# Twenty-six projection blocks of a hybrid layer computed as thirteen pairs of seven block products, with the gate pairs moved between the recurrence's heads

## The chip, the cores and the metric

The kernel runs as one program on one core of one Trainium2 chip. The core has five engines that take their instructions in order, each from its own queue: TensorE (PE, with its weight loads shown apart as PEld), VectorE (DVE), ScalarE (ACT), GpSimd (POOL) and SyncE (SP, which here only issues DMAs). They wait for one another through semaphores. The metric is the device time of one execution in microseconds (us), as the median of several runs.

## The reference

One residual layer over 512 tokens and 16 prepended meta tokens, model width 2048, all in float32.

```python
h = rms_norm(x, norm_g);  proj = h @ w_in          # w_in is 2048 x 12368
(q_a, k_a, v_a, z_a, q_i, k_i, w_i, q_b, f_b, i_b, z_b, gates) = split(proj)
...                                                 # branch A: indexer, top-128 keys per query, attention
y_a = o_a * silu(z_a)
qb = silu(q_b);  f = lb + (1 - lb) * sigmoid(f_b);  vb = i_b
o_b = hgrn2_chunkwise(qb, 1 - f, vb, log f)         # S_t = diag(f_t) S_{t-1} + k_t v_t^T, o_t = S_t^T q_t
y_b = rms_norm(o_b) * silu(z_b)
p = einsum('btnc,ncd->btnd', [y_a, y_b], w_branch)
out = x + sum_n(sigmoid(gates_n) * p_n) @ w_out
```

Branch B has 8 heads of 128 channels. Per head it needs one 128-column block each of q_b, f_b, i_b and z_b. The f and i blocks are needed for the meta tokens too (528 tokens), q and z for the 512 tokens alone.

## The kernel before, in words

**Layout.** The normalised input h is kept transposed in SBUF, 16 tiles of 128 channels by 528 tokens, each as a pair: hH (h rounded to the fast float32r format) and hL (the rest). Every weight chunk of 128 x 1024 numbers (`raw`, a 512 KB DMA on SP's queue; six buffers) is split in the same way into `wh` by an ACT copy and `wl` by a DVE subtraction (function `hi_lo`, three buffers of each). A product is then three matmuls per 128 x 128 weight block: hH with wh, hL with wh, hH with wl.

**Two kinds of projection.** A plain job (`Job`) makes one block of 128 output columns: 16 channel tiles x 3 matmuls of 512 tokens, or, where the meta tokens are needed (k, v, f, i), 16 x 3 matmuls of 264 tokens twice. A `Pair` makes two blocks together by a scheme in Winograd's form of Strassen's algorithm: the weight matrix of the two blocks is a 2 x 2 of sub-matrices (two output blocks by two halves of the channels, raw chunks 11, 21, 22, 12), the tokens are cut into two halves, and seven block products of 8 x 3 matmuls of 256 tokens replace eight. It needs four sums of weight chunks, s1 to s4 (`sum_1` ... `sum_4`), sums of the input halves (`tops_task`, once for all pairs, into the tiles TB; `place_t3` writes one more into h's own tiles), and five additions of products in `run_pair` (the p1, g1 and g2 tiles; PSUM banks px, py, pz, pw). Of the input projection only the merge gates are made in pairs (16 of them); the output projection is made in 8 pairs (`run_out`).

**Order.** One loop goes through the list `jobs`: indexer, z_a, k, v, q of attention, then per head of the recurrence q, f, i (24 plain jobs), then 8 plain z_b jobs, 16 gate pairs, 32 branch jobs, 8 output pairs. Everything that isn't a projection runs as generators (`ki_task`, `idx_task`, `topk_task`, `qa_task`, `pv_task`, `hgrn_task`, `gate_task`, `tops_task`): after every three matmuls of a plain job `pump` lets those continue whose results a small clock in the kernel's own planner (`Core`, costs in ns) holds to be ready. So the planner writes down one fixed order for each engine. Before the first gate pair all tasks are finished, and `run_pair` pumps none.

**The recurrence.** `hgrn_task` runs a head as a chain: transposes of v (bank phv), the diagonal product (phd), then seven levels. A level is 16 (at the end 8 and 4) small matmuls into the bank phl, then on DVE a predicated copy into `attn`, a product into k (`hk`), one into q (`QA`) and one into the decays (`TT`). The next level's matmuls wait for `hk` and `QA`. Then come the state products (phk, phs, `S`), the output (pho), its norm with a power on POOL (`hsq`), and in `gate_task` a transpose and the product with silu(z).

**Splits.** The chunk for product i+3 is split when product i is over, since three buffers stand in a ring; so it has the time of two products before PE needs it.

Of the kernel before, what the change touches and what calls it, by code (L numbers as in the profile page):

```python
# [16 lines left out]
D = 2048  # L17
# [20 lines left out]
LAT = 180.0  # L38
SAME = {"pe": 0.0, "act": 60.0, "dve": 125.0, "pool": 60.0}
MARGIN = 300.0  # L40


class Core:
# [63 lines left out]
    def ptt(self, out, a, b, op):  # L107
        self.nc.gpsimd.tensor_tensor(out, a, b, op=op)  # L108
# [66 lines left out]
def hybrid_kernel(ctx, tc, x, meta, vecs, w_in, rows, w_branch, w_out,  # L175
# [8 lines left out]
    S = Slots(E, sp, [f"s{i}" for i in range(67)], [128, T], None)  # L184
# [87 lines left out]
    vrow = cp.tile([35, 128], F32, name="vrow")  # L272
# [7 lines left out]
    RB = cp.tile([128, 192], F32, name="RB")  # L280
    tabA = cp.tile([128, 5, 64], F32, name="tabA")
    tabI = cp.tile([128, 5, 32], F32, name="tabI")
# [40 lines left out]
    class Pair:  # L323
# [3 lines left out]
        def __init__(self, kind, c0, c1, k0, k1, nk, ncols, n=0, done=None, more=()):  # L327
            self.kind, self.c0, self.n, self.done, self.nk, self.ncols = kind, c0, n, done, nk, ncols
            self.meta, self.pre, self.req, self.more = False, None, None, more
# [115 lines left out]
    def consts():  # L445
# [42 lines left out]

    def prep(half, kt):
# [42 lines left out]
    wi = cp.tile([128, 4, 16], F32, name="wi")  # L532
# [59 lines left out]
    def idx_task(j, xq):  # L592
# [50 lines left out]
        if not idx_left[0]:  # L643
            S.put(kkH, kkL, CQ, SQ)
# [100 lines left out]
    zs = {}  # L745
    yd = [[tc.dram_tile([128, 512], F32, name=f"yd{n}_{h}") for h in range(8)] for n in range(2)]

    def spill_y(n, h, s, e):
        yield e
        nc.sync.dma_start(yd[n][h], s[:, :512])  # L750
# [5 lines left out]
    def qa_task(h, xq, prev):  # L756
# [24 lines left out]
        for qt in (3, 2, 1, 0):  # L781
# [6 lines left out]
            else:  # L788
                pb = yield from bank("plg")
                parts = [(pb[:, :kq], slice(0, kq))]  # L790
                vs[qt] = pb[:, :kq]
# [10 lines left out]
        for qt in (3, 2, 1, 0):  # L802
# [5 lines left out]
            (B2 if kq > 512 else B1).put(pbs[qt])  # L808
# [12 lines left out]
    def pv_task(h, ps, e):  # L821
# [7 lines left out]
        po = yield from bank("pov")  # L829

# [15 lines left out]
        for b in (3, -1, 0, 1, 2):  # L846
# [13 lines left out]
            B1.put(pb)  # L860
            if b != 2:
# [15 lines left out]
        e = E.tt(zs[h][:, :512], po, zs[h][:, :512], OP.mult)  # L877
        B1.put(po)
        spawn(spill_y(0, h, zs[h], e), 0)
# [9 lines left out]
    AT = [None, None]  # L889
# [741 lines left out]
```

## Time and profile before

| | |
|---|---|
| median of 3 runs | 1587.43 us (1586.98 to 1587.56) |
| the profiled execution's own time | 1591.29 us |
| its span from the first instruction to the last | 1589.5 us |
| granted TensorE clock | 0.998 |
| busy: PE, PEld, DVE, ACT, POOL | 1569.0, 1425.6, 1058.0, 592.4, 73.0 us |
| heads of the recurrence (first q block to last head) | about 490 to 830 us |
| z_b jobs | about 830 to 928 us |
| 16 gate pairs | about 928 to 1246 us |
| branch jobs | about 1246 to 1426 us |
| output pairs | about 1426 to 1589 us |

In a group's row of the profile stand the line, the engine, the operation, what is written and read, and the count; then busy us, mean ns of one, idle time of the engine just before them, and what ended it. Line numbers are those of the kernel that ran; most operations are recorded by helpers, so one line (L104: DVE's tensor_tensor; L90 and L88: matmuls) stands for many places, and the tile names tell them apart.

### The profile page before, as it was taken

The numbers are of one execution on the slowest core, as the hardware profiler recorded it, in microseconds if no ns is written. First come the engines' busy times: TensorE is split into PE (matmuls) and PEld (weight loads), VectorE is DVE, ScalarE is ACT, GpSimd is POOL, SyncE is SP. The second block draws the span as 40 slices with busy tenths as digits, with TensorE's granted clock in tenths as the row PEclk, the third lists the DMA queues.
The fourth block names the chain that finished last, engine by engine and source line by source line (L and its number), as shares of the span: only waits on it lengthen the run. The fifth ranks groups of instructions, "written<-read, shape, count | busy, mean of one in ns | idle before, by whom it ended". The sixth has DMA issues, their size and how long they took to land.

```text
span 1589.5 us, 28143 instructions
## 1 busy us (share of the span) xinstructions
PE 1569.0 (99%) x11736; PEld 1425.6 (90%) x11736; DVE 1058.0 (67%) x1821; ACT 592.4 (37%) x922; POOL 73.0 (5%) x63
## 2 busy tenths in 40 slices
PE   7999999999999999999999999999999999999998
PEld 6888889998879888999997899999999888889998
DVE  6687899526665645444445887777777543779886
ACT  5555322334444322222222344444444331334332
POOL 3100000100000000000000000000000000002111
PEclk9999999999999999999999999999999999999999
DMA  9222333333223222323232434444445764444551
GB/s 256 80 67 80 86 102 85 90 82 86 61 67 93 69 80 67 81 67 80 68 80 80 120 99 133 132 134 132 134 126 139 233 198 136 144 130 142 163 161 55
DMA packets 277904, 175.76 MB, mean 111 GB/s; under 512 B 8660, under 2 KB 263136, under 8 KB 277776
## 3 DMA queue, kind: packets, MB, share of 16 engines
q1 hardware_dynamic: 272208, 167.58, 37.4%
q10 hardware_dynamic: 5504, 6.29, 1.2%
q8 instruction: 92, 1.51, 0.4%
q14 instruction: 36, 0.29, 0.1%
q0 software_dynamic: 64, 0.08, 0.0%
HBM read 157.16 MB, written 16.78 MB: 109 GB/s over the span
## 4 chain that ended last, share of the span: by engine, by line
PE 95%; DVE 2%; issue 1%; DMA 1%; ACT 1%; POOL 0%; SPq 0%; ACTq 0%; DVEq 0%
PE pg L90 58%; PE po L88 9%; PE px L88 6%; PE py L88 6%; PE pz L88 5%; PE pw L88 3%; PE phl L90 1%; PE psc L90 1%; PE plg L90 1%; PE pov L88 1%; PE pho L90 1%; PE ppt L94 1%; PE px L94 1%; DVE wl L104 0%; PE phd L90 0%
## 5 line engine op out<-in xcount | busy, mean ns | idle before, releaser
L104 DVE TENSOR_TENSOR wl<-raw,wh 128x1024 fp32r<-128x1024 f32 x276 | 340.6, 1234 | 208.2 <-ACT wh L98 207.8
L90 PE MATMUL pg<-hH,wh 128*128 128x264 f32 (+1 forms) x1392 | 478.2, 344 | 0.0
L98 ACT ACTIVATE wh<-raw 128x1024 fp32r<-128x1024 f32 x278 | 294.2, 1058 | 483.0 <-PE pg L90 243.5
L90 PE MATMUL pg<-hH,wl 128*128 128x264 f32 (+1 forms) x1392 | 464.3, 334 | 0.0
L90 PE MATMUL pg<-hL,wh 128*128 128x264 f32 (+1 forms) x1392 | 462.7, 332 | 0.0
L90 PEld LDWEIGHTS pg<-hH,wl 128*128 128x128 f32 x1392 | 261.7, 188 | 26.4
L90 PEld LDWEIGHTS pg<-hH,wh 128*128 128x128 f32 x1392 | 261.7, 188 | 22.1 <-ACT hv L98 0.2
L90 PEld LDWEIGHTS pg<-hL,wh 128*128 128x128 f32 x1392 | 262.2, 188 | 21.3
L88 PE MATMUL po<-wh,mh 128*128 128x256 f32 x896 | 159.1, 281 | 0.7 <-DVE xq L104 0.5
L88 PEld LDWEIGHTS po<-wh,mh 128*128 128x128 f32 x896 | 137.5, 189 | 1.1 <-DVE xq L104 0.7
L88 PE MATMUL po<-wl,mh 128*128 128x256 f32 x448 | 125.7, 281 | 0.0
L90 PE MATMUL pg<-yH,wh 128*128 128x512 f32 x256 | 101.1, 395 | 0.4 <-ACT yH L98 0.4
L90 PE MATMUL pg<-yL,wh 128*128 128x512 f32 x256 | 100.7, 393 | 0.4 <-DVE yL L104 0.3
L90 PE MATMUL pg<-yH,wl 128*128 128x512 f32 x256 | 100.8, 394 | 0.0
L88 PEld LDWEIGHTS po<-wl,mh 128*128 128x128 f32 x448 | 84.3, 188 | 0.2
L98 ACT ACTIVATE wh<-sum 128x1024 fp32r<-128x1024 f32 x48 | 51.0, 1062 | 84.7 <-DVE wl L104 24.8
L104 DVE TENSOR_TENSOR wl<-sum,wh 128x1024 fp32r<-128x1024 f32 x48 | 61.8, 1287 | 16.9 <-ACT wh L98 16.9
L88 PE MATMUL px<-hL,wh 128*128 128x256 f32 x256 | 72.3, 282 | 0.0
L88 PE MATMUL px<-hH,wl 128*128 128x256 f32 x256 | 72.2, 282 | 0.0
L88 PE MATMUL px<-hH,wh 128*128 128x256 f32 x256 | 71.9, 281 | 0.0
L108 POOL TENSOR_TENSOR xq<-xq,op 128x512 f32<-128x512 f32 x16 | 30.4, 1914 | 689.1 <-ACT op L98 671.8
L90 PEld LDWEIGHTS pg<-yL,wh 128*128 128x128 f32 x256 | 48.2, 188 | 12.2 <-DVE yL L104 1.1
(310 smaller groups left out, 2626.8 us busy)
## 6 DMA issues: line engine op xcount, KB each, us to landing
raw<-in_w_in_dram SPq DMA_DIRECT2D x192, 512.0 KB, 3.9
raw<-in_w_branch_dram SPq DMA_DIRECT2D x32, 512.0 KB, 4.3
raw<-in_w_out_dram SPq DMA_DIRECT2D x32, 512.0 KB, 3.6
gd<-gate SPq DMA_DIRECT2D x32, 256.0 KB, 4.3
g<-gd SPq DMA_DIRECT2D x30, 256.0 KB, 3.0
x<-in_x_dram SPq DMA_DIRECT2D x16, 256.0 KB, 5.7
xq<-in_x_dram ACTq DMA_DIRECT2D x16, 256.0 KB, 4.0
out_dram<-xq SPq DMA_DIRECT2D x15, 256.0 KB, 2.4
```

Of the source, the lines that this page charges most:

```text
L88: self.nc.tensor.matmul(out, lhsT, rhs, start=start, stop=stop, skip_group_check=True)
L90: self.nc.tensor.matmul(out, lhsT, rhs, start=start, stop=stop)
L94: self.nc.tensor.transpose(out, in_, ident)
L98: self.nc.scalar.activation(out, in_, f, **kw)
L104: self.nc.vector.tensor_tensor(out, a, b, op=op)
L108: self.nc.gpsimd.tensor_tensor(out, a, b, op=op)
```

## The change

- The q, f and i blocks of all eight heads and the last two z_b blocks are made in pairs by the seven products: f with i of one head (8 pairs, half width 264 tokens, since each half takes 8 meta tokens along), q with q of two heads (3 pairs), z with q (2 pairs). The first six z_b blocks stay plain jobs and come before them.
- The 16 gate pairs no longer follow the heads: two of them stand after each head's f and i pair. `run_pair` now pumps tasks after every three matmuls, and the tasks are no longer finished before the first pair; only `tops_task` is. It is cut in two, starts at the seventh q_a job of the attention in place of the fourth z_b job, and waits for free slots.
- h's columns are laid out as two halves of 264 tokens (8 meta and 256 others each), so plain jobs of 512 tokens read two stretches of 256.
- The weight sums s3 and s4 are no longer DVE additions but DMAs issued by POOL that add into the destination (`dma_add`), for all 37 pairs, the output's too; s4 is issued one product earlier than before.
- silu(z_a) and silu(z_b) are written to DRAM and read back (SP's queue) where they are used, and some tables share the general slots, of which there are 69 in place of 67.
- One `attn` tile in place of two; a pair of a head's q, f, i goes through SBUF (p1, g1, g2) instead of being read from PSUM.

```diff
+NSLOT = 69
+    def dma_add(self, out, a):
+        self.nc.gpsimd.dma_start(out, a, accum_op=OP.add)
+        return self.at("pool", 4000.0, [out], [out, a])
...
     def sum_3(pr):
             pr.s3 = pr.raw["21"]["raw"]
-            E.tt(pr.s3, pr.raw["11"]["raw"], pr.s3, OP.add)
+            E.dma_add(pr.s3, pr.raw["11"]["raw"])
     def sum_4(pr):
             pr.s4 = pr.raw["12"]["raw"]
-            E.tt(pr.s4, pr.s2, pr.s4, OP.add)
+            E.dma_add(pr.s4, pr.s2)
...
     def hgrn_task(h, prev):
         while (prev and not prev.done) or not all(t.done for t in qa_tasks):
             yield WAIT
+        while not all(i in hg[h] for i in ("q", "k", "v")):
+            yield WAIT
+        yield hg[h]["t"]
...
+        while len(S.free) < 3:
+            yield WAIT
...
     def gate_task(h, on):
-        while "z" not in hg[h]:
+        while not S.free or "z" not in hg[h]:
             yield WAIT
-        z = hg[h]["z"]
+        z = slot("hz")
+        nc.sync.dma_start(z[:, :512], zd[h])
...
-        yield e
+        yield e + 3000.0
...
     def d_za(h):
         def f(b):
-            zs[h] = silu_mul(b, "zs")
+            s = silu_mul(b, "zs")
+            spawn(spill(zad[h], s, E.clk["dve"] + LAT), 0)
...
+    def d_zp(h):
+        def f(g):
+            s, e = silu(g, "hz")
+            hg.setdefault(h, {})["z"] = 1
+            spawn(spill(zd[h], s, e), 0)
...
-    def tops_task():
+    def tops_task(i):
-        for k in range(8):
+        for k in range(4 * i, 4 * i + 4):
+            while len(S.free) < 8 + ROOM or k > 3 and k - 4 not in TB:
+                yield WAIT
...
     def run_pair(pr, nxt, late, last):
-        bk, W = {}, slice(0, 256)
+        w = pr.w
+        bk, W, V = {}, slice(0, w), slice(w, 2 * w)
...
             for k in range(8):
-                th, tl = TB[k][tn]
+                th, tl = (t[:, 264 - w:264] for t in TB[k][tn])
                 E.mm(b, op["h"][k], th, st_, False, loose=True)
                 E.mm(b, op["h"][k], tl, False, False, loose=True)
                 E.mm(b, op["l"][k], th, False, k == 7, loose=True)
+                pump()
...
-            elif i == 2:
+            if i == 1:
                 sum_4(pr)
...
-    for h in range(8):
-        jobs += [Job("in", C_QB + 128 * h, 128, done=d_qb(h)), Job("in", C_FB + 128 * h, 128, True, done=d_fb(h)),
-                 Job("in", C_IB + 128 * h, 128, True, done=d_ib(h))]
-    jobs += [Job("in", C_ZB + 128 * h, 128, done=d_zb(h)) for h in range(8)]
-    jobs[-5].pre = pre_t
+    jobs += [Job("in", C_ZB + 128 * h, 128, done=d_zb(h)) for h in range(6)]
+    jobs[-8].pre = pre_t
...
+    Q, Z = ([(c + 128 * h, d(h)) for h in range(8)] for c, d in ((C_QB, d_qb), (C_ZB, d_zp)))
+    first = [(Z[6], Q[0]), (Z[7], Q[1]), (Q[3], Q[2]), None, (Q[5], Q[4]), None, (Q[7], Q[6]), None]
+    gates = [(n, j) for n in range(2) for j in range(0, 16, 2)]
     for h in range(8):
+        if first[h]:
+            two(*first[h])
+        two((C_FB + 128 * h, d_fb(h)), (C_IB + 128 * h, d_ib(h)), w=264)
+        for n, j in gates[2 * h:2 * h + 2]:
+            c = C_G + D * n + 128 * j
+            two((c, d_gate(n, j, 256)), (c + 128, d_gate(n, j + 1, 0)), f=AF.Sigmoid)
...
-                for t in hg_tasks + on_tasks + t_task:
+                for t in t_task:
                     finish(t)
-                while tasks:
-                    finish(tasks[0])
```

The order of the built program shows the rest at three places. On DVE, at the middle levels of a head: before, in the fifth head, stand the level's four operations (`attn`, `hk`, `QA`, `TT`), and of the projection that runs beside them one product with the sigmoid (`hq`) and splits (`wl`):

```order
L942 COPY_PREDICATED attn_4863<-masks,phl_5282 128x32x8
L104 TENSOR_TENSOR hk_7013<-hk_7013,TT_7177 128x33x8
L104 TENSOR_TENSOR QA_7161<-QA_7161,TT_7177 128x32x8
L104 TENSOR_TENSOR TT_7177<-TT_7177 128x33
L104 TENSOR_TENSOR hq_7319<-pg_7144,hq_7319 128x512
L104 TENSOR_TENSOR wl_7325<-raw_6863,wh_7324 128x1024
L942 COPY_PREDICATED attn_4863<-masks,phl_5282 128x16x16
L104 TENSOR_TENSOR hk_7013<-hk_7013,TT_7177 128x16x16
L104 TENSOR_TENSOR QA_7161<-QA_7161,TT_7177 128x16x16
L104 TENSOR_TENSOR TT_7177<-TT_7177 128x16
L942 COPY_PREDICATED attn_4863<-masks,phl_5282 128x8x32
```

Now, in the same head, beside a gate pair (`p`, `g`: additions of products; `sum`: s1 and s2 of the next pair):

```order
L976 COPY_PREDICATED attn_6082<-masks,phl_6089 128x64x4
L106 TENSOR_TENSOR hk_10248<-hk_10248,TT_10310 128x66x4
L106 TENSOR_TENSOR QA_10282<-QA_10282,TT_10310 128x64x4
L106 TENSOR_TENSOR TT_10310<-TT_10310 128x66
L106 TENSOR_TENSOR g_546_10449<-p_539_10234,pz_10404 128x256
L106 TENSOR_TENSOR sum_150_10451<-sum_150_10396,raw_10078 128x1024
L106 TENSOR_TENSOR wl_10454<-raw_10078,wh_10453 128x1024
L976 COPY_PREDICATED attn_6082<-masks,phl_6089 128x32x8
L106 TENSOR_TENSOR hk_10248<-hk_10248,TT_10310 128x33x8
L106 TENSOR_TENSOR QA_10282<-QA_10282,TT_10310 128x32x8
L106 TENSOR_TENSOR TT_10310<-TT_10310 128x33
L106 TENSOR_TENSOR g_546_10449<-p_539_10234,pw_10457 128x256
```

Between two levels DVE now has an addition of products, a weight sum and a split, where it had at most a sigmoid product and a split.

On PE, at the turn of a product in a head's levels, stand before three matmuls of 512 tokens per channel tile (bank pg), and the level (phl) after nine of them:

```order
L90 MATMUL phl_5282<-QA_6231,hk_6083 32x16 x16
L90 MATMUL pg_6214<-hH_396,wh_6087 128x512
L90 MATMUL pg_6214<-hL_397,wh_6087 128x512
L90 MATMUL pg_6214<-hH_396,wl_6088 128x512
L90 MATMUL pg_6214<-hH_413,wh_6157 128x512
L90 MATMUL pg_6214<-hL_414,wh_6157 128x512
L90 MATMUL pg_6214<-hH_413,wl_6158 128x512
L90 MATMUL pg_6214<-hH_429,wh_6157 128x512
L90 MATMUL pg_6214<-hL_430,wh_6157 128x512
L90 MATMUL pg_6214<-hH_429,wl_6158 128x512
L90 MATMUL phl_5282<-QA_6231,hk_6083 32x16 x16
```

Now the level stands between the products of a gate pair (banks py, pz), matmuls of 256 tokens. The end of one such gap, in the fourth head:

```order
L90 MATMUL py_9152<-hH_388,wh_9137 128x256
L90 MATMUL py_9152<-hL_389,wh_9137 128x256
L90 MATMUL py_9152<-hH_388,wl_9138 128x256
L90 MATMUL py_9152<-hH_412,wh_9137 128x256
L90 MATMUL py_9152<-hL_413,wh_9137 128x256
L90 MATMUL py_9152<-hH_412,wl_9138 128x256
L90 MATMUL pz_9306<-tT_4606,wh_9188 128x256
L90 MATMUL pz_9306<-tT_4607,wh_9188 128x256
L90 MATMUL pz_9306<-tT_4606,wl_9189 128x256
L92 MATMUL phl_6089<-QA_9184,hk_9150 32x16 x16
```

From the first level of that head to the last, the six gaps hold 21, 18, 30, 27, 18 and 21 of these matmuls.

On POOL stand, in the stretch of the heads and gate pairs, before only the powers of the heads' norms, one for each head:

```order
L108 TENSOR_TENSOR hsq_6579<-hsq_6579,mhalf 128x4
L108 TENSOR_TENSOR hsq_7044<-hsq_7044,mhalf 128x4
L108 TENSOR_TENSOR hsq_7509<-hsq_7509,mhalf 128x4
L108 TENSOR_TENSOR hsq_7974<-hsq_7974,mhalf 128x4
L108 TENSOR_TENSOR hsq_8439<-hsq_8439,mhalf 128x4
```

Now the adding DMAs of two weight sums for every pair stand among them (`raw<-raw`: s3 of the next pair; `raw<-sum`: s4 of the running one):

```order
L110 TENSOR_TENSOR hsq_7651<-hsq_7651,mhalf 128x4
L115 DMA raw_7338<-raw_7283 128x1024
L115 DMA raw_7539<-sum_110_7709 128x1024
L115 DMA raw_7679<-raw_7629 128x1024
L115 DMA raw_7818<-sum_114_7946 128x1024
L115 DMA raw_7917<-raw_7882 128x1024
L115 DMA raw_8047<-sum_118_8176 128x1024
L115 DMA raw_8147<-raw_8112 128x1024
L115 DMA raw_8275<-sum_122_8485 128x1024
L110 TENSOR_TENSOR hsq_8749<-hsq_8749,mhalf 128x4
```

So between the powers that two heads' norms wait for, POOL here issues eight such DMAs.

More of the change, by code (lines that the diff above doesn't have):

```diff
@@ L183, in hybrid_kernel @@
     E = Core(nc)
-    S = Slots(E, sp, [f"s{i}" for i in range(67)], [128, T], None)
+    S = Slots(E, sp, [f"s{i}" for i in range(NSLOT)], [128, T], None)
     B1 = Slots(E, pp, [f"b{i}" for i in range(6)], [128, 512], None)
@@ L487, in hybrid_kernel, with halves, tok @@
     hH, hL = [], []
+    def halves(a):
+        return a[:, :528].rearrange("p (a b) -> p a b", a=2)
+    def tok(b):
+        o = 128 * b + (8 if b < 2 else 16)
+        return slice(o, o + 128)
     def prep(half, kt):
@@ L788, in qa_task @@
             else:
-                pb = yield from bank("plg")
-                parts = [(pb[:, :kq], slice(0, kq))]
-                vs[qt] = pb[:, :kq]
+                if qt:
+                    pb = yield from bank("plg")
+                vs[qt] = pb[:, :kq] if qt else pb[:, KQ[1]:KQ[1] + kq]
+                parts = [(vs[qt], slice(0, kq))]
             pbs[qt] = pb
@@ L888, in hybrid_kernel @@
     on_tasks = []
-    AT = [None, None]
+    AT = []
+    zd = [tc.dram_tile([128, 512], F32, name=f"zd{h}") for h in range(8)]
     MT = cp.tile([128, 256], F32, name="MT")
+    VM = [cp.tile([128, 16], F32, name=f"VM{i}") for i in range(2)]
     LB = []
@@ L1199, in run_pair @@
             if i == 2:
-                g1, g2 = slots("gate", 2)
-                pr.done(0, g1[:, W], b, None)
+                g1 = main_slot("g1")
+                E.act(g1[:, W], b, pr.f)
                 B1.put(bk["x"])
             elif i == 5:
-                late.append(lambda g=g2: pr.done(1, g[:, :512], g[:, :512], g))
+                late.append(lambda g=g2: pr.done[1](g))
             elif i == 6:
-                late.append(lambda g=g1: pr.done(0, g[:, 256:512], g[:, 256:512], g))
+                late.append(lambda g=g1: pr.done[0](g))
             if last:
@@ L1398, in pre_t @@
     def pre_t():
-        t_task.append(spawn(tops_task(), 2))
+        t_task.extend(spawn(tops_task(i), 2) for i in range(2))
     def req_br(n, p):
@@ L1512, in hybrid_kernel @@
     for ji, job in enumerate(jobs[2:], 3):
-        need[0] = 1 + jobs[ji].meta if ji < len(jobs) else 0
+        need[0] = 1 + (jobs[ji].meta or "pair" in (job.kind, jobs[ji].kind)) if ji < len(jobs) else 0
         if job.pre:
@@ L1517, in hybrid_kernel @@
             job.req()
-        if job.kind == "gate":
+        if job.kind == "pair":
             npair += 1
             if npair == 1:
-                for t in hg_tasks + on_tasks + t_task:
+                for t in t_task:
                     finish(t)
-                while tasks:
-                    finish(tasks[0])
                 late += [lambda: place_t3(0), lambda: place_t3(4)]
@@ L1545, in hybrid_kernel @@
             b = B1.get("pg")
[L1546 removed]
+            parts = [(b[:job.ncols, :], slice(0, 512))]
+            if job.kind == "in":
+                parts = [(b[:job.ncols, :].rearrange("p (a b) -> p a b", a=2), None)]
         for ch in job.chunks:
@@ L1555, in hybrid_kernel @@
                 for o, c in parts:
-                    mm3(o, ch, kk_, kt, mh[:, c], ml[:, c], kt == 0, kt == job.kts - 1)
+                    u, v = (t[:, c] if c else halves(t)[:, :, 8:264] for t in (mh, ml))
+                    mm3(o, ch, kk_, kt, u, v, kt == 0, kt == job.kts - 1)
                 pump()
```

183 lines of the change are left out of this document (108 added, 75 removed).

## The prediction

> **What bounds the kernel now.** I read the page's busy times and its chain first:
>
> ```profile
> PE 1569.0 (99%) x11736; PEld 1425.6 (90%) x11736; DVE 1058.0 (67%) x1821; ACT 592.4 (37%) x922; POOL 73.0 (5%) x63
> PE 95%; DVE 2%; issue 1%; DMA 1%; ACT 1%; POOL 0%; SPq 0%; ACTq 0%; DVEq 0%
> PE pg L90 58%; PE po L88 9%; PE px L88 6%; PE py L88 6%; PE pz L88 5%; PE pw L88 3%; PE phl L90 1%; PE psc L90 1%; PE plg L90 1%; PE pov L88 1%; PE pho L90 1%; PE ppt L94 1%; PE px L94 1%; DVE wl L104 0%; PE phd L90 0%
> ```
>
> The chain is PE at 95%, and 58% of it is the plain jobs (pg). A busy PE can hide waits, since matmuls overlap, so I read the stages next (busy us of PE, PEld, DVE, ACT, POOL, then clock, DMA share, GB/s):
>
> ```profile
> 420.00:490.00 70.00, 66.00 (x361) 55.59 (x361) 42.56 (x116) 31.74 (x65) 4.79 (x6) 1.00 0.27 75
> 530.00:830.00 300.00, 299.42 (x3258) 272.17 (x3257) 152.61 (x320) 76.39 (x127) 7.06 (x7) 1.00 0.28 74
> 830.00:928.00 98.00, 98.00 (x621) 78.80 (x621) 71.10 (x131) 28.41 (x42) 1.01 (x1) 1.00 0.34 95
> 928.00:1246.00 318.00, 318.00 (x2689) 317.90 (x2688) 239.94 (x265) 143.79 (x186) 0.00 (x0) 1.00 0.50 137
> 644.00:655.00 11.00, 11.00 (x90) 10.76 (x89) 2.77 (x4) 2.11 (x5) 1.01 (x1) 1.00 0.37 97
> ```
>
> The gate pairs (928 to 1246) are 16 x 168 = 2688 matmuls of 256 columns in 318.0 us: 0.118 us each and no gap. 644 to 655 holds only f and i matmuls of 264 columns: 11.0/90 = 0.122 us. For 512 columns I take an unbroken run from the chain in order of time (start, us, what):
>
> ```profile
> 859.92 11.10 PE pg L90 x48
> 614.68 0.38 PE phl L90 x32
> ```
>
> 11.10/48 = 0.231 us. So PE is dense, its time is a count of matmuls times these three spacings, and DVE is the next engine: 75% in the gate pairs, 51% in the heads.
>
> **The change, part by part.** *Matmuls.* The plain jobs' forms:
>
> ```profile
> L90 PE MATMUL pg<-hH,wh 128*128 128x512 f32 x624 | 253.8, 407 | 0.0
> L90 PE MATMUL pg<-hH,wh 128*128 128x264 f32 x768 | 224.4, 292 | 0.0
> ```
>
> Ten blocks of 512 columns leave (8 q, 2 z: 48 matmuls each, 480) and sixteen blocks at 264 (8 f, 8 i: 96 each, 1536). Eight pairs at 264 come (8 x 168 = 1344) and five at 256 (840). That is -480 x 0.231 = -110.9, -1536 x 0.122 = -187.4, +1344 x 0.122 = +164.0, +840 x 0.118 = +99.1: **-35.2 us**. The heads' and the attention's own matmuls stay as many. This is the gain's ceiling, since nothing else leaves PE.
>
> The Trainium skill's "TensorE: Matmul & The Clock Gate", section "Back-to-back issue gap", speaks against it: the spacing of load and matmul pairs hardly falls with the width there, 131 ns at 512 columns and 81 at 128, so 98 at 256 by a straight line, my estimate. By that the sum would be about 0 (-63 - 152 + 133 + 82). The rows above, 231 against 118 ns, disagree with it: halving the columns halves the spacing.
>
> *DVE beside the heads.* The same rows for DVE, of the heads (first four) and of the gate pairs:
>
> ```profile
> L942 DVE COPY_PREDICATED attn<-masks,phl 128x256 f32<-128x256 uint8 x49 | 25.6, 522 | 28.6 <-PE phl L90 28.4
> L104 DVE TENSOR_TENSOR hk<-hk,TT 128x264 f32<-128x264 f32 x21 | 9.2, 438 | 0.0
> L104 DVE TENSOR_TENSOR QA<-QA,TT 128x256 f32<-128x256 f32 x42 | 17.5, 417 | 0.0
> L104 DVE TENSOR_TENSOR TT<-TT 128x66 f32<-128x66 f32 x7 | 1.5, 221 | 0.0
> L104 DVE TENSOR_TENSOR wl<-raw,wh 128x1024 fp32r<-128x1024 f32 x80 | 97.8, 1223 | 43.6 <-ACT wh L98 43.6
> L104 DVE TENSOR_TENSOR raw<-raw,raw 128x1024 f32<-128x1024 f32 x16 | 19.5, 1220 | 0.0
> L104 DVE TENSOR_TENSOR sum<-raw,raw 128x1024 f32<-128x1024 f32 x15 | 18.2, 1214 | 0.0
> L104 DVE TENSOR_TENSOR gate<-p,pz 128x256 f32<-128x256 f32 x31 | 13.0, 421 | 4.6 <-PE pz L88 0.6
> ```
>
> A level costs DVE 0.52 + 0.44 + 0.42 + 0.2 = 1.6 us. With the split and the addition beside it (1.22 + 0.42) it is 3.2, and with one of the sums s1 and s2 4.5. These overlap a little: the gate stage's DVE rows add up to 250 us for 239.9 busy, so times 0.96: 3.1 and 4.3. PE has, by the new order, 21, 18, 30, 27, 18 and 21 matmuls of 0.118 us between levels, and 0.38 us for a level: about 2.9, 2.6, 4.0, 3.6, 2.6 and 2.8 us. DVE needs in the gaps from the second on about 2.7 (no addition falls there), 4.3, 4.3, 3.1 and 3.1: 17.5 against 15.6. It falls 1.9 us behind, less the lead that the first gap leaves (2.9 against a level's 1.4 without TT, less the two signals: about 1). PE then waits at phl about 1 us a head, where it waited for nothing before. Bounds: 0 if the lead is larger, 2 if there is none. I take 1: **+8 us**, 0 to +16. The splits themselves don't stall PE: each has two products, 5.7 us, for 1.06 on ACT and 1.22 on DVE.
>
> *The first pairs' inputs.* `tops_task` moves from the z stage into the attention's end. Its largest DVE row and the wait that shows how tight the attention's chain is:
>
> ```profile
> L104 DVE TENSOR_TENSOR tr<-hH,hL 128x512 f32<-128x512 f32 x16 | 10.3, 683 | 0.0
> L90 PEld LDWEIGHTS plg<-kTH,qH 128*128 128x128 f32 x40 | 7.5, 188 | 5.1 <-DVE pS L104 4.7
> ```
>
> For each of the eight steps two tr of 0.68 us, four of 0.42 and splits of 0.69 and 0.42 make 4.2 us, 34 in all, into some 125 us (eight plain jobs and the attention's last heads) where DVE was at 42.56/70 = 61%: 88% now. There PE already lost 4.7 us to DVE (pS), before the plg of three heads. And the last two steps stand in the last plain z job, 11.1 us, in which DVE gets two steps, two sums, three splits and two sigmoid products: 8.4 + 2.4 + 3.7 + 1.4 = 16. The first product needs none of these inputs (2.8 us) and part may run ahead. I take **+3** for both, 0 to +8.
>
> *Weight sums by DMA.* It takes 2 x 1.22 us a pair off DVE, which is in the 4.3 above. The trace has no adding DMA. The nearest rows:
>
> ```profile
> raw<-in_w_in_dram SPq DMA_DIRECT2D x192, 512.0 KB, 3.9
> gd<-gate SPq DMA_DIRECT2D x32, 256.0 KB, 4.3
> g<-gd SPq DMA_DIRECT2D x30, 256.0 KB, 3.0
> ident<-in_ident_dram POOLq DMA_DIRECT2D x1, 64.0 KB, 4.2
> ```
>
> A plain 512 KB load lands in 3.9 us; an add reads two such tiles and writes one, so 3.9 to 3 x 3.9 = 11.7 us; I take 6, nearer the single load, because a plain load's 3.9 us holds its reading and its writing already. When is it due? s3 can start when s1 of the next pair is done, 1.8 us after product 3 (0.42 + 1.22 and signals), and is split four products (11.4 us) after product 3: 9.6 us free. s4 can start when chunk 12 is split, 2.7 us into the pair (1.06 + 1.22 and signals), and is itself split 11.4 us in: 8.7 us free. PE needs either two products later, less 2.6 us for the split: another 3.1, so 11.8 to 12.7 in all. At 6 us, and even at 11.7, PE doesn't wait: **0**. Above 9 us ACT and DVE would be held, which the heads' levels feel. If it costs nothing, it is because two to four products lie over it.
>
> The "DMA: Bandwidth & Descriptors" page of the Trainium skill, section "Anatomy of one DMA — SWDGE (gpsimd) path", gives 2.0 us plus bytes/436e3 per us for a POOL-issued DMA: 3.2 for 512 KB, 4.4 if both inputs count, an estimate. The sum by it stays the same; no run here shows such a DMA yet.
>
> On POOL's queue stand, behind a waiting add, the powers of the heads' norms, and ahead of s3 in the output's pairs its additions:
>
> ```profile
> L108 POOL TENSOR_TENSOR hsq<-hsq,mhalf 128x4 f32<-128x4 f32 x8 | 8.1, 1009 | 338.5 <-DVE hsq L116 338.5
> L108 POOL TENSOR_TENSOR xq<-xq,op 128x512 f32<-128x512 f32 x16 | 30.4, 1914 | 689.1 <-ACT op L98 671.8 <-issue 9.4 <-DVE op L104 7.5
> ```
>
> By the order each add's inputs are ready before a power (1.0 us) is asked for. Two of the additions (3.8 us) end about 1.7 products after product 3, which leaves s3 6.5 us until its split and 9.6 until PE: covered at 6 us.
>
> *z through DRAM and slots.* 32 transfers of 256 KB, 3.0 us to read back by the g row. The read is issued two to three products' time ahead in a head (the planner allows 3 us) and some 6 us ahead in the attention, behind at most one weight load on SP: 0, at worst 1 us for each of 16 reads on DVE.
>
> Sum: -35.2 + 8 + 3 = **-24** us on the profiled execution's 1591.29, so 1567. Its span is 1589.5, with 1.8 us around it; the median of the runs shown lies 3.9 lower, so I predict **1563.5 us**.
>
> **The rivals.** *No lag (13%):* the lead covers the levels, as in the heads now, where PE's weight loads for phl lost 0.8 us to QA in all:
>
> ```profile
> L90 PEld LDWEIGHTS phl<-QA,hk 128*32 128x32 f32 x1408 | 16.6, 112 | 15.4 <-issue 13.2 <-DVE QA L104 0.8
> ```
>
> That gives 1587.4 - 35 to -31, 1552 to 1556. Against it: 4.3 us of DVE beside 3.6 to 4.0 of PE. *More lag (13%):* 2 us a head and the ends of the bounds, or adds of 9 to 12 us that hold DVE: -35 + 16 + 4 to 9, 1573 to 1582. *Slower (9%):* the adds take more than 12.5 us, with contention on queues at 50% share or a slow add. Then every one of 74 adds holds PE by the excess, and -24 is gone from 74 x 0.33: from 12.8 us on the kernel is slower; at 14 us it is 1563.5 + 74 x 1.5 = 1675. For it: nothing in the trace shows the price; against it: even three plain loads in a row end sooner. *No gain (5%):* the seven products cost as much as the eight, or waits eat the whole: 1584 to 1590. The TensorE page's rule would end here; the spacings leave it 1 in 100 of these.
>
> **How the numbers follow.** The forecast, 1556 to 1573, has 60%. The range takes in no lag and more lag to the bound: **1551 to 1582**. A measurement tells 0.2% (3.2 us) from no change here. Faster: 60 + 13 + 13 = 86%; same 5%; slower 9%.
>
> **What would show it.** Plain pg matmuls fall by 480 and 1536, and the 13 pairs keep 0.118 to 0.122 us a matmul. Idle time before phl should be released by DVE's QA or hk, about 8 us; idle before px, py, pz, pw by wl near 0. An add's time to landing should be 4 to 9 us, with no wait of PE behind a wh made from raw or sum. I am wrong if the pairs' matmuls with weights from an added chunk wait, if the first pair starts late by more than 8 us, or if pairs beside heads run wider spacings.

## The result and the profile after

The changed kernel takes 1562.82 us (median of 4 runs, 1561.99 to 1563.86) where the kernel before, on the same chip, takes 1587.31 (4 runs, 1586.98 to 1587.56): a ratio of 0.9846, 95% interval 0.9829 to 0.9863. The prediction was 1563.5. The profiled execution of the changed kernel took 1562.53 us (span 1560.8), that of the kernel before 1591.29 (span 1589.5), so the profiles lie 28.8 apart and the medians 24.5. Some 3 us of the 28.8 are no gain. Here are the same 14 us near the start of the kernel before and of the changed kernel (busy us of PE, PEld, DVE, ACT, POOL, clock, DMA share, GB/s):

```profile
15.00:29.00 14.00, 13.04 (x68) 10.75 (x69) 9.08 (x19) 6.68 (x15) 6.38 (x7) 0.76 1.04 291
15.00:29.00 14.00, 13.12 (x88) 10.57 (x87) 11.86 (x25) 9.61 (x23) 7.25 (x6) 1.00 1.10 313
```

The work is the same there, but in its profiled execution the kernel before had a granted clock of 0.76 and made 20 matmuls fewer. By the starts of the first hundred matmuls that cost it 2.9 us. The profiles of the two experiments below that are built on the kernel before have a clock of 1.00 in this stretch.

The page's busy times and its chain, of the changed kernel:

```profile
PE 1539.4 (99%) x11904; PEld 1419.1 (91%) x11904; DVE 1102.5 (71%) x1903; ACT 634.9 (41%) x997; POOL 135.1 (9%) x136
PE 96%; DMA 1%; ACT 1%; DVE 1%; issue 0%; POOL 0%; SPq 0%; ACTq 0%; POOLq 0%
PE pg L92 39%; PE py L90 11%; PE pz L90 10%; PE px L90 10%; PE po L90 10%; PE pw L90 5%; PE phl L92 1%; PE psc L92 1%; PE pho L92 1%; PE pov L90 1%; PE plg L92 1%; ACT wh L100 1%; PE ppt L96 1%; PE phs L92 1%; DMA raw<-in_w_branch_dram 1%; PE px L96 1%
```

PE is still the chain; plain jobs (pg) fell from 58% of the span to 39%, and the pairs' banks took their place. The plain jobs' forms, and two stretches by engine (columns as above): all pairs of the heads and gates, and one gate pair with no head beside it.

```profile
L92 PE MATMUL pg<-hH,wh 128*128 128x512 f32 x464 | 187.3, 404 | 0.0
L92 PE MATMUL pg<-hH,wh 128*128 128x264 f32 x256 | 74.0, 289 | 0.0
```

```profile
553.60:1214.10 660.50, 657.90 (x6704) 645.78 (x6704) 485.02 (x741) 277.30 (x390) 57.75 (x67) 1.00 0.68 160
644.80:664.60 19.80, 19.80 (x170) 19.80 (x169) 13.35 (x15) 8.79 (x11) 1.70 (x2) 1.00 0.84 203
```

The first form stood at 624 and 768; times three, 480 and 1536 matmuls have gone. A pair still takes 19.8 us for its 168 matmuls, 0.118 us each, though the DMA engines are 84% busy there, where the gate pairs before had 50%.

To see where the time went I took, for every matmul of PE in the trace, the time from its start to the next start, and took off the three spacings of the prediction (0.231, 0.122, 0.118 us) wherever a plain or a pair matmul runs. From the first pqa to the first matmul of the branch stage this gives, in us:

| | before | after | difference |
|---|---|---|---|
| plain and pair matmuls, count times spacing | 758.9 | 723.7 | -35.2 |
| heads' own matmuls and the gaps ahead of them | 64.6 | 69.9 | +5.3 |
| attention's own matmuls and the gaps ahead of them | 54.5 | 52.0 | -2.5 |
| other time between plain and pair matmuls | 13.2 | 14.6 | +1.4 |
| branch stage | 179.3 | 183.1 | +3.8 |
| the stage ahead | 355.2 | 353.9 | -1.3 |
| the output | 163.8 | 163.4 | -0.4 |

The first row takes the prediction's own spacings, so it confirms the counts alone. The spacings of the pairs hold by the traces: 0.118 us at 256 columns and 0.122 at 264, beside heads too. The plain matmuls of 512 tokens did change. An unbroken run of 21 of them in the stage ahead, before and after (start, us):

```profile
114.50 4.82 PE pg L90 x21
111.67 4.89 PE pg L92 x21
```

In three traces of the order before they start 231.9 ns apart in that stage, in three of the changed order 234.2 ns; those of 264 tokens keep 123.2. They are the ones that now read h in two stretches of 256; no run has that change alone, so the cause is not shown. In all it makes some 1.8 us for the 771 of them in the stage ahead and 1.2 for the 621 behind it, which is most of the "other time" of +1.4. Without the half clock of the one profile the stage ahead would thus be 1.9 us longer after the change (by the starts from the hundredth matmul on), not 1.3 shorter.

Beside the count stand terms of a few us each. The waits of PE name two of them, the branch stage and the heads (engine and line, what was waited for, us in all, times, longest):

```profile
PE pg L92 <- ACT yH L100: 3.1, 1, 3.1
PE phs L92 <- ACT MT L100: 1.5, 8, 0.3
PE phl L96 <- ACT wh L100: 1.1, 1, 1.1
```

None of them is a wait of phl for QA or hk, on which the prediction had put 8 us. The adding DMAs (KB each, median us from issue to landing), beside the plain loads:

```profile
raw<-in_w_in_dram SPq DMA_DIRECT2D x192, 512.0 KB, 4.3
raw<-raw POOLq DMA_DIRECT2D x37, 512.0 KB, 5.3
raw<-sum POOLq DMA_DIRECT2D x37, 512.0 KB, 5.9
```

### The profile page after: what moved, and what is told of

The parts are those of the page before. It is cut to its first block, busy times and chain, and to the rows that moved or that the text cites. A ratio compares the mean times of both kernels' runs of the same rounds, so it can differ in the third digit from the quotient of the medians.

```text
span 1560.8 us, 29032 instructions
## 1 busy us (share of the span) xinstructions
PE 1539.4 (99%) x11904; PEld 1419.1 (91%) x11904; DVE 1102.5 (71%) x1903; ACT 634.9 (41%) x997; POOL 135.1 (9%) x136
## 4 chain that ended last, share of the span: by engine, by line
PE 96%; DMA 1%; ACT 1%; DVE 1%; issue 0%; POOL 0%; SPq 0%; ACTq 0%; POOLq 0%
PE pg L92 39%; PE py L90 11%; PE pz L90 10%; PE px L90 10%; PE po L90 10%; PE pw L90 5%; PE phl L92 1%; PE psc L92 1%; PE pho L92 1%; PE pov L90 1%; PE plg L92 1%; ACT wh L100 1%; PE ppt L96 1%; PE phs L92 1%; DMA raw<-in_w_branch_dram 1%; PE px L96 1%
## 5 line engine op out<-in xcount | busy, mean ns | idle before, releaser
L92 PE MATMUL pg<-hH,wh 128*128 128x512 f32 (+1 forms) x720 | 261.3, 363 | 0.0
L92 PE MATMUL pg<-hH,wl 128*128 128x512 f32 (+1 forms) x720 | 256.4, 356 | 0.0
L92 PE MATMUL pg<-hL,wh 128*128 128x512 f32 (+1 forms) x720 | 256.1, 356 | 0.0
L92 PEld LDWEIGHTS pg<-hH,wl 128*128 128x128 f32 x720 | 135.4, 188 | 20.9
L92 PEld LDWEIGHTS pg<-hH,wh 128*128 128x128 f32 x720 | 135.9, 189 | 16.6
L92 PEld LDWEIGHTS pg<-hL,wh 128*128 128x128 f32 x720 | 135.5, 188 | 16.0
L100 ACT ACTIVATE wh<-sum 128x1024 fp32r<-128x1024 f32 x74 | 78.5, 1061 | 139.9 <-PE pw L90 50.4
L90 PE MATMUL px<-hH,wh 128*128 128x256 f32 (+1 forms) x464 | 134.4, 290 | 0.0
L90 PE MATMUL px<-hH,wl 128*128 128x256 f32 (+1 forms) x464 | 131.0, 282 | 0.0
L90 PE MATMUL px<-hL,wh 128*128 128x256 f32 (+1 forms) x464 | 130.6, 282 | 0.0
L90 PEld LDWEIGHTS px<-hH,wh 128*128 128x128 f32 x464 | 87.5, 189 | 0.6
```

The costliest lines, as they stand in the source:

```text
L90: self.nc.tensor.matmul(out, lhsT, rhs, start=start, stop=stop, skip_group_check=True)
L92: self.nc.tensor.matmul(out, lhsT, rhs, start=start, stop=stop)
L100: self.nc.scalar.activation(out, in_, f, **kw)
```

## The experiments

All times are medians. A difference between kernels is the difference of their gains, each over the runs of the kernel before made beside it: 24.5 us for the changed kernel. By the intervals of the ratios such a difference is uncertain by some 3 us.

**Is VectorE at its edge beside a head?** In head 3's levels VectorE runs like this (start, us; changed kernel):

```profile
861.80 0.43 DVE L976 COPY_PREDICATED attn<-masks,phl 128x256 f32<-128x256 uint8 x1
862.13 0.43 DVE L106 TENSOR_TENSOR hk<-hk,TT 128x264 f32<-128x264 f32 x1
862.48 0.42 DVE L106 TENSOR_TENSOR QA<-QA,TT 128x256 f32<-128x256 f32 x1
862.81 0.22 DVE L106 TENSOR_TENSOR TT<-TT 128x66 f32<-128x66 f32 x1
862.95 0.42 DVE L106 TENSOR_TENSOR g<-p,pz 128x256 f32<-128x256 f32 x1
863.28 1.22 DVE L106 TENSOR_TENSOR sum<-sum,raw 128x1024 f32<-128x1024 f32 x1
864.42 1.22 DVE L106 TENSOR_TENSOR wl<-raw,wh 128x1024 fp32r<-128x1024 f32 x1
865.55 0.43 DVE L976 COPY_PREDICATED attn<-masks,phl 128x256 f32<-128x256 uint8 x1
```

There is no idle time, but each row starts 0.08 to 0.1 us before the one above has ended: a level with a split, a sum and an addition takes 865.55 - 861.80 = 3.75 us, where its durations add up to 4.36. By the starts of QA and phl in the trace, VectorE ends a level's QA 0.2 to 1.15 us before PE comes for it. Two kernels load VectorE further. The first makes s3 and s4 on VectorE, at the same places:

```diff
-        self.nc.gpsimd.dma_start(out, a, accum_op=OP.add)
+        self.nc.vector.tensor_tensor(out, a, out, op=OP.add)
```

> The order of every engine is kept, but both sums s3 and s4 of all 37 pairs are made by VectorE in place of the adding DMA. Theory (VectorE is at its edge beside a head: in the changed kernel's trace it runs from 856.6 to 869.6 us without a gap, and its QA products end only 0.2 to 0.65 us before PE's phl from the third level on): one to two sums of 1.14 us spacing fall into the levels of a head, less a lead of 0.2 to 0.5, so PE waits 0.7 to 2 us a head: 6 to 16 us slower than the changed kernel, 1569 to 1579, with waits of phl for QA. Rival (VectorE has room, since phl never waited for it): at most 3 us slower, 1562 to 1566. A third case, that the adding DMAs themselves hold something: faster than 1562.

Measured: 1570.31 us (before 1587.28), 7.5 slower than the changed kernel.

```profile
PE phl L92 <- DVE QA L106: 4.4, 8, 0.6
```

The wait is there, once in each head; 1.9 us more are lost in the first pair (21.8 us from its start to the next pair's, against 19.9). The second makes each level's copy into attn twice:

```diff
             E.dve([at], [pb], 256, lambda v: v.copy_predicated(
...
+            nc.vector.copy_predicated(
+                at[:, :512].rearrange("p (b w m) -> p b w m", w=2, m=m)[:, :, 1, :],
+                masks[:, 256 * li:256 * li + 256].rearrange("p (b m) -> p b m", m=m),
+                pb.rearrange("p (b m) -> p b m", m=m))
```

> Beside each of the 56 levels VectorE makes the copy into attn a second time (0.43 to 0.74 us by its rows, some 0.33 to 0.6 by the spacing of starts, 2.9 us a head); the order of all else is kept. Theory (VectorE has no gap between the third level and the seventh of a head and a lead of 0.2 to 0.65 us over PE): the excess over the leads goes to PE, 0.8 to 2.2 us a head: 6 to 18 us slower than the changed kernel, 1569 to 1581, with PE waiting at phl for QA. Rival (PE didn't wait at phl because VectorE has room): within 3 us, 1561 to 1566.

Measured: 1577.10 (before 1588.02), 13.6 slower.

```profile
PE phl L92 <- DVE QA L106: 9.9, 24, 0.6
```

Some 2.9 us a head are added and 1.7 come back as time (1.9 in this profile, by the table's method): the lead covers the rest. Both runs say the same: VectorE is full beside a head, and just not late.

**What do the adding DMAs do, and how late may they be?** First alone, in the kernel before:

```diff
-            E.tt(pr.s3, pr.raw["11"]["raw"], pr.s3, OP.add)
+            E.dma_add(pr.s3, pr.raw["11"]["raw"])
-            E.tt(pr.s4, pr.s2, pr.s4, OP.add)
+            E.dma_add(pr.s4, pr.s2)
```

> The kernel before with one part of the change alone: s3 and s4 of its 24 pairs by adding DMA in place of VectorE. Theory (the additions stand on no path there: VectorE is 75% busy in the gate pairs, and a sum by DMA that takes 5.3 to 5.9 us is free up to 11.6): no change, 1584 to 1590. Rival A (the adding DMAs bring a good part of the 24.5 us): 1575 to 1583. Rival B (in pairs that follow each other without a head between, the sums are due earlier than 5.9 us): above 1592, with PE waiting for weights from added tiles.

Measured: 1588.05 (11 runs; before 1588.02, 15 runs), ratio 0.9998, interval 0.9989 to 1.0007. Where no head stands beside the pairs they bring nothing; in the new order they bring the 7.5 us above. Then they were made late, by one and by two hops through DRAM (hops holds one tile of DRAM, or two):

```diff
+        src = a
+        for d in hops:
+            self.nc.gpsimd.dma_start(d, src)
+            src = d
-        self.nc.gpsimd.dma_start(out, a, accum_op=OP.add)
+        self.nc.gpsimd.dma_start(out, src, accum_op=OP.add)
```

> Each of the 74 adding DMAs takes its input by way of DRAM: one plain DMA of 512 KB out, then the adding one, which waits for it; about 10 us from the first issue to the sum, where it was 5.3 to 5.9. Theory (slack as the prediction put it: 8.7 to 9.6 us until ScalarE and VectorE are held, 11.8 to 12.7 until PE waits): the splits made from s4 come 1 to 2 us late, PE itself doesn't wait in the plain pairs and loses up to 1 us a head where VectorE is full: 0 to 12 us slower than the changed kernel, 1563 to 1575. Rival A (the adds are nearly due as they are, the slack is 6 us): 74 times 4 us, some 300 us slower. Rival B (slack is far larger than put): no change, within 2 us.

Measured: 1578.55 (before 1587.28), 15.8 slower, beyond the theory's 12. The DMA issues and PE's waits in the output stage:

```profile
raw<-hop POOLq DMA_DIRECT2D x74, 512.0 KB, 5.5
hop<-raw POOLq DMA_DIRECT2D x37, 512.0 KB, 6.1
hop<-sum POOLq DMA_DIRECT2D x37, 512.0 KB, 6.0
```

```profile
PE po L90 <- ACT wh L100: 6.6, 3, 2.7
PE po L90 <- DVE wl L106: 3.1, 4, 0.9
```

At 11.6 us to the sum, the 29 pairs of heads and gates keep their times to the tenth (19.9, 20.5, 24.1, 25.4 us), and each of ScalarE's 389 instructions beside them starts within 0.22 us of its old place. So neither PE nor ScalarE's splits were held there, not even past the 8.7 to 9.6 us that the prediction allowed until a split. All is lost in the output's pairs. Each of the three waits for wh follows an s4 whose first hop stands right behind an addition of POOL of 1.85 us (xq at 1469.00, the hop at 1470.80, PE waits until 1483.78). That this order makes it late is read off the rows; no run changes it. And more is lost than waited for: 17 us between output matmuls, with 9.7 of waits. The rest is the clock after a wait (columns as above, four stretches of 4 us):

```profile
1432.00:1436.00 4.00, 3.14 (x28) 2.94 (x26) 0.00 (x0) 0.00 (x0) 3.90 (x4) 1.00 0.79 131
1436.00:1440.00 4.00, 1.86 (x8) 1.67 (x9) 2.76 (x4) 2.00 (x2) 0.87 (x1) 0.72 0.42 157
1440.00:1444.00 4.00, 4.00 (x20) 4.00 (x20) 3.83 (x5) 1.18 (x2) 0.56 (x1) 0.50 1.04 259
1444.00:1448.00 4.00, 4.00 (x34) 4.00 (x33) 1.75 (x2) 1.86 (x2) 0.00 (x0) 0.92 1.03 340
```

PE waits 2.1 and 0.9 us, and then runs some 20 matmuls in 4 us at a granted clock of 0.50, where the row behind it has 34. The Trainium skill's "TensorE: Matmul & The Clock Gate", section "Part 1: The HAM clock gate", has this: the clock falls to half once a window of about 3.4 us was idle, and comes back after one busy window. The 0.50 agrees; here it came after two waits close together, neither as long as such a window.

> As the run with one hop, with a second plain DMA from DRAM to DRAM between: about 15 us to the sum. Theory (PE waits from 11.8 us for s4 and from about 14 us for s3): 37 x 3.2 + 37 x 1 = 155 us slower than the changed kernel, 90 to 250 by how long the hops take, with PE waiting for weights that are split from an added tile. Rival A (slack 6 us): some 670 us slower. Rival B (slack is far larger, above 15 us): within 5 us of the changed kernel.

Measured: 1746.03 (before 1587.28), 183 slower; hops and add take 5.9 or 6.8, 4.2 and 5.3 us, 15.4 to 16.3 in all.

```profile
PE po L90 <- ACT wh L100: 45.3, 12, 9.3
PE px L90 <- ACT p L100: 28.2, 15, 3.4
PE pz L90 <- DVE g L106: 24.6, 8, 5.9
```

```profile
552.80:1313.50 760.70, 693.56 (x6704) 673.52 (x6703) 481.24 (x741) 274.05 (x390) 120.54 (x179) 0.96 0.78 217
```

Now the pairs wait too: their stage takes 760.7 us for the same 6704 matmuls, 100 more, at a clock of 0.96. In the heads' and gates' pairs the free time of an add thus lies between 11.6 and 15.4 us, which holds the prediction's 11.8 to 12.7, and the kernel uses 5.3 to 5.9 of it.

**Does the count carry the gain?** The five pairs of q and z become ten plain jobs again, the rest stays. The pairs write t3 over half of eight input tiles, which the plain q and z blocks behind the first pair then read, so those blocks' values are not the reference's; work and order are as meant.

```diff
-            two(*first[h])
+            jobs += [Job("in", c, 128, done=d) for c, d in first[h]]
-    first = [(Z[6], Q[0]), (Z[7], Q[1]), (Q[3], Q[2]), None, (Q[5], Q[4]), None, (Q[7], Q[6]), None]
+    first = [(Z[6], Q[0], Z[7], Q[1]), None, (Q[3], Q[2]), None, (Q[5], Q[4]), None, (Q[7], Q[6]), None]
```

> The five pairs of the eight q blocks and two z blocks are plain jobs again, at their places between the heads; the f and i pairs, the gate pairs and the adding DMAs stay. Theory (only the count of matmuls by their spacings matters): +480 x 0.231 - 840 x 0.118 = 11.8 us slower than the changed kernel, 1572 to 1578. Rival A (load and matmul pairs cost nearly the same whatever their width, 131 against 98 ns): 19 us faster, 1540 to 1550. Rival B (pairs of 256 columns beside heads cost more than their count, by VectorE and banks): less than 6 us slower, 1563 to 1569.

Measured: 1576.07 (before 1588.02), 12.5 slower; the count said 11.8.

**The new wait at the branch stage.** PE waits 3.1 us for yH at 1218 us. The rows around it, of SP, DVE and ACT (changed kernel; a q behind an engine's name marks its DMA issues):

```profile
1203.13 9.08 SPq L362 DMA_DIRECT2D raw<-in_w_branch_dram  x3
1216.85 0.34 SPq L1057 DMA_DIRECT2D hz<-zd  x1
...
1219.57 0.75 DVE L127 SCALAR_TENSOR_TENSOR hz<-pht,cvec,hz 128x512 f32<-128x512 f32 x1 [2.67 <-DMA hz<-zd]
1220.24 0.41 DVE L106 TENSOR_TENSOR g<-p,pz 128x256 f32<-128x256 f32 x1
...
1220.68 0.42 ACT L100 ACTIVATE g<-g 128x256 f32<-128x256 f32 x1 [4.58 <-DVE g L106]
1221.01 1.13 ACT L100 ACTIVATE yH<-yr 128x512 fp32r<-128x512 f32 x2
```

Head 7's z is read from DRAM behind three weight loads on SP, whose queue stands 4.6 us until the last of them has landed, and lands itself at 1219.5; VectorE waits at hz, behind it stands the last pair's sum, behind that the sigmoid on ScalarE, behind that the last two yH, and PE waits for those. Behind the wait the clock is down as well:

```profile
1222.00:1228.00 6.00, 5.72 (x19) 4.51 (x19) 0.99 (x2) 1.20 (x2) 0.00 (x0) 0.72 0.81 263
```

So one kernel reads head 7's z earlier:

```diff
         S.put(vt, qa, ss)
+        if h == 7 and "z" in hg[h]:
+            zq.append(slot("hz"))
+            nc.sync.dma_start(zq[0][:, :512], zd[h])
         yield e
```

> The read of head 7's z from DRAM is issued when that head's output product is, some 14 us earlier, ahead of the weight and y loads on SP's queue; nothing else changes. Theory (the new wait of PE at the start of the branch products, 3.1 to 5 us near 1218 us, hangs on that read: VectorE sat 2.7 us at hz until it landed at 1219.5, and behind it stood a sum of the last gate pair, the sigmoid on ScalarE and the last two yH): 3 to 4.5 us faster than the changed kernel, 1558 to 1560, and the wait at the start of the branch stage at 1 to 2 us as in the kernel before. Rival (the y loads, which start late because their slots come free late, set it): no change, within 1 us.

Measured: 1556.61 (before 1587.28), 6.2 faster than the changed kernel; ratio 0.9806, interval 0.9792 to 0.9821.

```profile
PE pg L92 <- ACT yH L100: 0.2, 1, 0.2
```

That is more than the 3 to 4.5 expected. In this profile 4.0 us are gone in the branch stage: the wait of 3.1, and what the clock took behind it. 1.1 are gone in the stage ahead, where PE waits 7.0 us for the first load and not 8.3. The output, where nothing was changed, is 1.1 shorter, spread evenly over its matmuls, and it is 0.4 to 1.1 shorter in the four kernels below that are built on this one. I can't lay either to the edit.

The other heads' reads of z are late as well, only PE doesn't feel it. In the changed kernel VectorE waits at every one, and the read lands in 6.5 us by the median:

```profile
DVE hz L127 <- DMA hz<-zd: 13.5, 8, 2.7
```

**The attention.** The inputs of the pairs are now made beside its end, and yet it is 2.5 us shorter in the table. The diff has a small edit that the prediction passed over: the logits of a head's first query block (qt = 0) use the free half of the bank of the block before. It was undone in the kernel with z read early:

```diff
-                if qt:
-                    pb = yield from bank("plg")
-                vs[qt] = pb[:, :kq] if qt else pb[:, KQ[1]:KQ[1] + kq]
+                pb = yield from bank("plg")
+                vs[qt] = pb[:, :kq]
```

> The kernel with head 7's z read early, in which the logits of an attention head's first query block have a PSUM bank of their own again (plg for qt = 0), as in the kernel before, in place of the free half of the block before's. Theory (this sharing, and nothing of the added work, took away the three waits of 1.3 to 1.6 us that PE had there for pS of VectorE): they come back, 3 to 5 us slower than that kernel's 1556.6, 1559 to 1562, with plg waiting for pS. Rival (the order around the attention took them away): within 1.5 us of 1556.6.

Measured: 1565.49 (before 1588.03), 8.1 slower than with the shared bank, more than either theory had.

```profile
PE pov L90 <- DVE pTL L106: 3.6, 2, 2.7
PE plg L92 <- DVE pTL L106: 1.5, 1, 1.5
PE ppt L96 <- DVE qay L106: 1.5, 1, 1.5
PE plg L92 <- DVE pS L106: 1.3, 1, 1.3
```

And it was made alone in the kernel before (the lines above with their signs turned):

> The kernel before with one part of the change alone: the logits of an attention head's first query block in the free half of the bank of the block before's. Theory (PE's three waits of 1.3 to 1.6 us at plg for pS there are waits for a free bank): they go, 3 to 6 us faster than the kernel before, 1581 to 1585. Rival (the sharing pays only beside the added making of inputs): within 1.5 us of 1587.3.

Measured: 1583.82 (before 1588.58), 4.8 faster; ratio 0.997, interval 0.9959 to 0.9981. The waits of plg for pS, 4.0 us in the profile before, are gone:

```profile
PE plg L90 <- DVE pTL L104: 0.6, 1, 0.6
```

So the shared bank is worth 4.8 us by itself and 8.1 in the new order. The difference of 3.3 lies within the intervals of the two, and a part of the 8.1 is the clock, which is down to 0.66 from 510 to 515 us, behind the wait of 2.7 us for pTL. What the added work costs the attention is better read by the table's method: 54.5 us in the kernel before, 50.4 there with the bank shared, 52.0 in the changed kernel, 58.9 with the bank of its own again. So it costs 1.6 us with the shared bank, and 4.4, clock included, without it.

**Could more blocks go into pairs, and does the place of the gates matter?** Both in the kernel with z read early. Two more z blocks as a pair:

```diff
-    jobs += [Job("in", C_ZB + 128 * h, 128, done=d_zb(h)) for h in range(6)]
+    jobs += [Job("in", C_ZB + 128 * h, 128, done=d_zb(h)) for h in range(4)]
-    first = [(Z[6], Q[0]), (Z[7], Q[1]), (Q[3], Q[2]), None, (Q[5], Q[4]), None, (Q[7], Q[6]), None]
+    first = [(Q[1], Q[0]), None, (Q[3], Q[2]), (Z[5], Z[4]), (Q[5], Q[4]), (Z[7], Z[6]), (Q[7], Q[6]), None]
```

> The kernel with head 7's z read early, and blocks z4 and z5 too as a pair between the heads (six pairs of q and z blocks in place of five). Theory (counts): -96 x 0.231 + 168 x 0.118 = 2.4 us faster than that kernel's 1556.6: 1553 to 1556. Rival (two plain jobs fewer, 22 us, leave the attention's tail and the making of the first pairs' inputs uncovered): 1558 to 1575, with gaps of PE before the first pair's products.

Measured: 1566.58 (before 1588.02), 9.2 slower than with z4 and z5 plain. The first pair takes 28.9 us in place of 19.9, waiting for its inputs and then at a lower clock (0.57 from 541.5 to 549.5 us):

```profile
PE py L90 <- ACT tT L100: 4.4, 2, 2.6
```

Then the gates behind all heads, in a loop of their own behind the one over the heads:

```diff
-        for n, j in gates[2 * h:2 * h + 2]:
+    for n, j in gates:
```

> The kernel with head 7's z read early, with the 16 gate pairs behind all heads, as the kernel before had them, in place of two behind each head; all products and adding DMAs stay. The 13 pairs of f, i, q and z give 263 us of cover, 33 us a head beside its own 10; a head takes 33 to 35 us from phv to pho as it is. Theory (the gates between the heads only give cover, and the same splits and sums stand beside a level either way): within 6 us of that kernel's 1556.6. Rival A (the heads' chain no longer fits, since it needs the gates' products as cover): 1570 to 1620, with PE idle between heads. Rival B (the interleaving costs by itself, through VectorE): 1540 to 1550.

Measured: 1561.00 (before 1588.03), 3.6 slower: within the 6 us, though the intervals of the two kernels' ratios touch (0.9792 to 0.9821 and 0.9814 to 0.9843). The trace shows a wait that the kernel with z early doesn't have:

```profile
PE phl L92 <- DVE QA L106: 4.0, 9, 0.7
```

By the table's method the heads take 73.1 us there, and 70.0 with the gates between. So heads that follow each other without a pause leave VectorE less time to catch up, and the gate pairs between them are worth some 3 to 4 us.

**The last wait, on ScalarE.** Of the heads' +5.3, 4.7 stand at phs (the gap ahead of it and its own spacing, eight heads) and 1.3 at the first transpose of v in the first head, and there alone (the wait of 1.1 for wh above); phl is 0.5 shorter. The split wh<-sum, 1.06 us, stands ahead of the copies MT and kd on ScalarE. One more kernel, on top of the early z, has phs come later, by what the task yields behind kd's copy:

```diff
-        yield e
+        yield e + 700.0
```

> The kernel with head 7's z read early, in which the planner holds each head's phs products 0.7 us longer after ScalarE's copies MT and kd, so that they stand two groups of three matmuls later in PE's order. Theory (phs costs 4.7 us more in the changed kernel than before, 0.59 a head, because the split of a sum, wh<-sum of 1.06 us, stands ahead of MT and kd on ScalarE): 3 to 4.7 us faster than that kernel's 1556.6, 1552 to 1554. Rival (what follows, S on VectorE and pho, is then late in its place): no gain, within 1 us.

Measured: 1553.64 (5 runs; before 1588.58), 4.3 faster than the kernel with z early alone, and 0.978 of the kernel before, interval 0.9767 to 0.9793: faster than both kernels of this case. In its trace phs has no gap ahead of it and its old spacing again, 4.7 us less, and nothing behind it became late.

## Why the prediction was right, and where it was not

- **Matmuls, -35.2:** right in the counts, by the trace, and in price, by the q and z blocks put back (12.5 for 11.8). What it left out is that the plain matmuls of 512 tokens that stay start some 2 ns further apart, 3.0 us over all of them. The spacing rule of the Trainium skill's "TensorE: Matmul & The Clock Gate", section "Back-to-back issue gap", had this at about 0 by the prediction's estimate; 0.118 us at 256 columns and 0.231 at 512 decide against it here, beside heads too.
- **VectorE behind in the levels, +8:** the step failed by size. The mechanism is real (1.7 us a head come with 2.9 us more work) but sits just beyond what the kernel asks. The term that was wrong is the factor 0.96 between durations and time taken. It came from a stage with idle time in it, where VectorE was busy for 239.9 of 318 us; in a dense stretch it is 3.75/4.36 = 0.86, so a level with a split and a sum needs 3.75 us and not 4.3. (By its own figures the gaps on PE add up to 15.4 us, not 15.6, which makes little difference.) Phl waited 0. That is the rival "no lag" in mechanism, though not in its time.
- **What stood in its place, not foreseen:** ScalarE, +4.7 at phs, shown by the last experiment, and +1.3 at the first head, read off a wait alone. The prediction counted only VectorE's work beside a head; an order that is full puts ScalarE's splits ahead of small copies too.
- **Inputs of the pairs, +3:** between the 1.6 and the 4.4 that the added work costs with the shared bank and without it, and right that the cover there is thin: two jobs fewer cost 9.2. But the term shown in the profile is -2.5, because the shared bank, which the prediction did not price, gives more back. The row of plg with pS 4.7, which it quoted for the tight chain, was the row of that bank.
- **Adding DMAs, 0:** right, with 5.3 and 5.9 us for an assumed 6, and the bound of 11.8 to 12.7 us until PE waits fits the runs. Its 9 us until ScalarE and VectorE are held was too short: at 11.6 us ScalarE's splits beside the heads kept their places. In the output's pairs, which wait first, it is s4 that comes late, and the prediction had looked at s3. The priced loss, the excess times the number of adds, is too small once PE stops, since the clock falls as well. By the Trainium skill's "DMA: Bandwidth & Descriptors", section "Anatomy of one DMA — SWDGE (gpsimd) path", 3.2 or 4.4 us were to be had by an estimate; the rows have 0.9 to 2.7 us more.
- **z through DRAM, 0:** wrong by 4.0 at one of the 16 reads. The prediction took 3.0 us for a read and at worst 1 us of VectorE each; the reads of silu(z_b) land in 6.5 us, and VectorE waits 1.7 us at each of the eight on average. PE feels the last alone. The prediction left out what is queued behind VectorE at the end of the last pair, and the three weight loads ahead on SP. Why the reads take 6.5 us is open: with the sums on VectorE they take 4.1.
- **Profile against median, -3.9:** right to take off. Most of it was the half clock near the start of that one execution, so the gain to compare with the sum's 24 is not the profiles' 28.8 but some 26 without that stretch, or the 24.5 of the medians.
- **The hit within 0.7 us:** luck in part. Against the sum, the heads cost 2.7 less (5.3 for 8) and the attention 5.5 less (-2.5 for +3). The branch stage (3.8), the stage ahead (1.9) and the other time (1.4), which the sum had at nothing, cost 7.1 more. The range, not the hit, is what the working had earned.
- **The rivals' sums:** "more lag" adds up to -15 to -10, so 1572 to 1577; the 1582 at its end doesn't follow from its terms. Nothing hangs on it here.

Open: what the wider spacing of the plain matmuls comes from, and why the output is 0.4 to 1.1 us shorter in the kernels with z read early.

## What to carry to other kernels

Where one engine is dense, price the others by the distance between starts in a dense stretch, not by durations or by the busy time of a stage, and count every engine that a step passes through, the one with small copies too. A read that PE doesn't feel fifteen times can be on its path the sixteenth, so look at the place where a stage ends. Before you compare two profiles, compare the granted clock stage by stage: one stretch at half clock in one of them passes for a gain. And read a diff for the edits that free a buffer: a wait that a profile puts down to another engine's work may be a wait for a bank.

## What the runs showed of the hardware

An adding DMA of 512 KB from SBUF to SBUF lands in 5.3 to 5.9 us, 1.0 to 1.6 more than a plain load of the same size in the same kernel (4.3), and with 74 of them the pairs' matmuls keep their 0.118 us. A wait of PE can cost more than itself: after 2.1 and 0.9 us the granted clock was 0.50 for the next 4 us, after one of 3.1 us it was 0.72 over 6 us, and in the output 9.7 us of waits became 17. The plain matmuls of 512 columns start 234.2 ns apart in the changed kernel, where they read h in two stretches of 256, and 231.9 ns in the kernel before, where they read one. VectorE starts an instruction 0.08 to 0.1 us before the one ahead has ended, when neither waits, so that seven rows take 0.86 of their durations' sum.
